# Wider tile slots, product corrections issued before the norm, and head weights applied by TensorE

## The chip, the cores and the metric

One NeuronCore of a Trainium2 chip runs the whole kernel in one launch. The metric is the device time of an execution in microseconds (us). Engines are named as the profile does: PE (TensorE matmuls), PEld (its weight loads), DVE (VectorE), ACT (ScalarE), POOL (GpSimd), SP (the queue that issues most DMAs). L260 is line 260 of the kernel before.

## The reference, cut to what matters

Two blocks of a transformer, then a third with other attention and a mixture of experts; 512 tokens, width 1024, all in float32. What the change touches is the normalisation that opens most stages, and the index scores of the sparse attention (`dsa_mixer`):

```python
def layer_norm(x, g, b):
    mu = jnp.mean(xf, axis=-1, keepdims=True)
    var = jnp.mean(jnp.square(xf - mu), axis=-1, keepdims=True)
    return (xf - mu) * lax.rsqrt(var + LN_EPS) * g + b
...
# sparse attention, block of 128 queries: 8 index heads of width 64
logits = jax.nn.relu(jnp.einsum('bthd,bsd->bths', qib, ki))
score = jnp.einsum('bths,bth->bts', logits, wb)
score = jnp.where(causal[None], score, -jnp.inf)
_, idx = lax.top_k(score, topk)          # topk = 128 of 512 keys
# softmax attention (8 heads of 128, 2 of keys and values) over those keys alone
```

## The kernel before, in words

Activations are kept transposed, eight tiles of 128 channels by 512 tokens. A float32 value is split into two rounded parts, `hi` and `lo`, and a product is made of three matmuls (`mm3`, L260 to L262: hi by hi, hi by lo, lo by hi). Weights come by DMA into `wr`, ACT casts them to `wh` (L237) and DVE, or POOL where the caller says so, subtracts to get `wl` (L238). Both are rings of six tiles. Everything else lies in slots of one pool, `a` (`t()`, 53 slots, 2 x 258 x 4 = 2064 bytes rounded up to a multiple of 32, 2080), small things in `s`, and PSUM has eight banks `p`.

The stages are: feed-forward (`ffn`), mixer, feed-forward, per-layer embedding (`ple`), twice over; then the third block (`nsa` and the experts). The mixers are `ab` (convolution and state space) and `c_mixer` (sparse attention). Six of these stages (ab, ffn, ple, c_mixer, ffn, ple) open with `first_products`: the first four products of the stage are made from values that are multiplied by the gain, but not normalised yet, together with two more columns (hence 258), while DVE works out mean and deviation. `normed` (L402 to L405) then normalises the eight tiles: two DVE operations L402, ACT's L403 and cast L404, DVE's L405 for the low part. Lines L434 (ACT) and L435 to L437 (DVE) correct the four products by the rows of mean and deviation. In the code `normed` is called inside the loop over k, ahead of the corrections. Below, T is the time at which the last matmul of the first products of a site ends.

In `c_mixer` the index queries `qi` (four tiles, two heads in each) and index keys `ki` go through `rope` (a shuffle L959, three elementwise operations L961 to L963, of which POOL makes the first, `engs[0]`). `index()` then makes for j = 3, 2, 1 the scores of 128 queries against 128(j+1) keys: eight matmuls of 64 rows (L1029, even heads on the upper half of the rows, odd heads on the lower), ACT's relu (L1031), and DVE multiplies by the head's weight and adds up (L1033, L1035), and adds the causal mask (L1036). Then 16 rounds of MAX and MATCH_REPLACE (L1042, L1043) over the three score tiles find the top 128, while PE makes the products of ten heads (`product`). `probs` (L1117 to L1134) makes the softmax, and L1557 transposes it. The lows of the last seven head weights and of the first four `cout` weights are made by POOL.

The build's scheduler sets the order of the instructions on each engine; an engine works through its own list in that order, and a waiting instruction holds up all behind it.

Of the kernel before, what the change touches and what calls it, by code (L numbers as in the profile page):

```python
# [18 lines left out]
P = 128  # L19
# [28 lines left out]
V_LNG, V_LNB, V_CONV, V_S5D, V_BGLU, V_NMIX, V_NFFN, NVEC = 0, 48, 96, 108, 112, 116, 124, 132  # L48
C_ID, C_TT, C_TRI, C_CM, C_SGN, C_INVA, C_INVI, C_SINA, C_SINI, C_N = 0, 128, 256, 384, 512, 513, 514, 515, 516, 576
C_I32, C_BASE, C_TOK, C_I128 = 640, 672, 736, 768  # L50
SLOTS, RING, S5_STEP, HALF = 53, 6, 2, 258
CAP, NCOL, NPAIR, NEXT = 64, 32, 16, 16
SLOPES = [float(np.float32(2.0 ** (-8.0 * i / 16))) for i in range(1, 17)]

# [85 lines left out]
class K:  # L140
    def __init__(self, ctx, tc, A, out, stop=None, taps=None):
        self.nc, self.tc, self.A, self.out, self.stop, self.taps = tc.nc, tc, A, out, stop, taps or {}
        nc = tc.nc
        self.n = self.rooms = 0
        self.act = ctx.enter_context(tc.tile_pool(name="act", bufs=1))
        self.ps = ctx.enter_context(tc.tile_pool(name="ps", bufs=1, space=PSUM))
        self.dram = ctx.enter_context(tc.tile_pool(name="dram", bufs=1, space=bass.MemoryType.DRAM))
        self.const = self.act.tile([P, CONST_COLS], F32, name="const", tag="const", bufs=1)
        self.vec = self.act.tile([P, NVEC], F32, name="vec", tag="vec", bufs=1)
        self.ident = self.const[:, C_ID:C_ID + P]  # L150
        self.ones = self.act.tile([P, P], F32, name="ones", tag="ones", bufs=1)
        nc.vector.memset(self.ones, 1.0)
        self.half_pi = self.act.tile([P, 1], F32, name="half_pi", tag="half_pi", bufs=1)
        nc.vector.memset(self.half_pi, math.pi / 2)
        self.vec_hi, self.vec_lo = (self.act.tile([P, V_CONV], F32R, name=n, tag=n, bufs=1) for n in ("vec_hi", "vec_lo"))
        self.background = iter(())

    def begin(self):

        nc, A = self.nc, self.A  # L160
        X, H = [self.t() for _ in range(DT)], self.pairs()
        raw = [self.wide() for _ in range(4)]
        hi, lo = ([self.act.tile([P, 1024], F32R, name=self.nm(t), tag=t, bufs=RING) for _ in range(4)] for t in ("whi", "wlo"))

        def load(t, src):
            with self.after(self.loaded):
                nc.sync.dma_start(t, src)
            self.loaded = self.mark()

        def x(d):  # L170
            load(X[d], A["xT"][d])
            nc.scalar.copy(H[d][0], X[d])
            nc.gpsimd.tensor_tensor(H[d][1], X[d], H[d][0].bitcast(F32), ALU.subtract)

        def w(n, h):
            c = slice(h * S, h * S + S)
            load(raw[n][:, c], A[("w1", "w3")[n % 2]][0, n // 2][:, c])
            nc.scalar.copy(hi[n][:, c], raw[n][:, c])
            nc.vector.tensor_tensor(lo[n][:, c], raw[n][:, c], hi[n][:, c].bitcast(F32), ALU.subtract)

        self.loaded = self.mark()
        x(0)
        w(0, 0)
        w(1, 0)
        x(1)
        w(2, 0)
        w(3, 0)
        x(2)
        x(3)
        x(4)  # L190
        for n in range(4):
            w(n, 1)
            if n < 3:
                x(5 + n)
        with self.after(self.mark()):
            nc.gpsimd.dma_start(self.vec, A["vec"])
            nc.gpsimd.dma_start(self.const, A["const"])
            nc.gpsimd.tensor_copy(self.vec_hi, self.vec[:, :V_CONV])
            nc.gpsimd.tensor_tensor(self.vec_lo, self.vec[:, :V_CONV], self.vec_hi.bitcast(F32), ALU.subtract)
        return X, H, list(zip(hi, lo))  # L200

# [12 lines left out]
        return self.act.tile([P, 1024], F32, name=self.nm("wr"), tag=tag, bufs=2 if tag == "wraw2" else 4)  # L214

    def sm(self, n, dt=F32, p=P):
        t = self.act.tile([P, 64], dt, name=self.nm("s"), tag="s", bufs=34)
        return t[:p, :n]

    def old(self, j):  # L220
# [155 lines left out]

    def halves(self, t):

        return t.rearrange("p (h c) -> p h c", c=HALF)[:, :, :256]

    def gained(self, y, g, b=None):

        nc = self.nc
        if b is None:
            hi, lo = self.t(F32R), self.t(F32R)
            hv, lv, yv = hi, lo, y
        else:
            hi, lo = self.t(F32R, (P, 2 * HALF)), self.t(F32R, (P, 2 * HALF))
            hv, lv, yv = self.halves(hi), self.halves(lo), y.rearrange("p (h c) -> p h c", c=256)
            for t, v in ((hi, self.vec_hi), (lo, self.vec_lo)):  # L390
                nc.gpsimd.tensor_copy(t[:, 256:HALF], v[:, g:b + 1:b - g])  # L391
        gain = self.vec[:, g:g + 1]
        nc.scalar.activation(hv, yv, AF.Copy, scale=gain)  # L393
        nc.vector.scalar_tensor_tensor(lv, yv, gain, hv.bitcast(F32), op0=ALU.mult, op1=ALU.subtract)
        return hi, lo
# [12 lines left out]
    def first_products(self, ws, norm):  # L408

        nc = self.nc
        Y, G, st, g, b = norm
        first, second = [self.bank() for _ in ws], [self.bank() for _ in ws[::2]]
        place = lambda i: second[i // 2][:, i % 2 * 256:i % 2 * 256 + 256]
        for k in range(DT):
            s = slice(k * P, (k + 1) * P)
            hi, lo = G[k]
            for i, w in enumerate(ws):
                l = (w[0][:, s], w[1][:, s])  # L420
                self.mm3(first[i][:, :HALF], l, (hi[:, :HALF], lo[:, :HALF]), k == 0, k == DT - 1)
                self.mm3(place(i), l, (hi[:, HALF:HALF + 256], lo[:, HALF:HALF + 256]), k == 0 and i % 2 == 0, k == DT - 1 and i % 2 == 1)
            self.last_mm = self.mark()
            if k == 0:
                self.loaded = self.mark()
            if k == 1:
                rm = self.result(self.rstd(self.sums(st, range(4), True), 4, 1e-5, True))
            if k == 4:
                rows = [self.spread(c) for c in rm]
                H = self.normed(Y, rows, g, b)  # L430
        res = []
        for i in range(len(ws)):
            c, t = self.sm(2), self.t()
            nc.scalar.copy(c, first[i][:, 256:HALF])  # L434
            nc.vector.tensor_tensor(t[:, :256], first[i][:, :256], rows[0][:, :256], ALU.mult)  # L435
            nc.vector.tensor_tensor(t[:, 256:], place(i), rows[0][:, 256:], ALU.mult)
            nc.vector.scalar_tensor_tensor(t, rows[1], c[:, 0:1], t, op0=ALU.mult, op1=ALU.add)  # L437
            res.append((t, c[:, 1:2]))
        return res, H

    def pairs(self):
        return [(self.t(F32R), self.t(F32R)) for _ in range(DT)]
# [533 lines left out]
    def c_mixer(self, X, H):  # L976
# [9 lines left out]
        def dense(w):  # L986
            o = self.bank()
            self.dense(o, w, H)
            return o

        for _ in self.rounds([self.rope(lambda j=j: first[j] if j < 4 else dense(cw(j)), ri, sh_i, P, (nc.gpsimd, nc.vector), qi, j) for j in range(5)], 1):
            pass
        ki = qi.pop()

# [26 lines left out]
        def index():  # L1021
            for j in (3, 2, 1):
                n = (j + 1) * P
                acc = self.t()[:, :n]
                for h in range(8):
                    o = self.bank()
                    rs = slice(64 * (h % 2), 64 * (h % 2) + 64)
                    q = qi[h // 2]
                    nc.tensor.matmul(o[:, :n], q[rs, j * P:(j + 1) * P], ki[rs, :n], start=True, stop=True)  # L1029
                    r = self.t()  # L1030
                    nc.scalar.activation(r[:, :n], o[:, :n], AF.Relu)  # L1031
                    if h == 0:
                        nc.vector.tensor_scalar(acc, r[:, :n], wi[j][:, h:h + 1], None, op0=ALU.mult)  # L1033
                    else:
                        stt(acc, r[:, :n], wi[j][:, h:h + 1], acc, op0=ALU.mult, op1=ALU.add)  # L1035
                tt(acc[:, n - P:n], acc[:, n - P:n], cm, ALU.add)  # L1036
                bias[j] = acc
                yield
            for i in range(16):
                for acc in bias[:0:-1]:  # L1040
                    m8 = self.sm(8)
                    nc.vector.max(m8, acc)  # L1042
                    nc.vector.match_replace(acc, m8, acc, -3e38)  # L1043
                yield
            for acc in bias[:0:-1]:
                nc.vector.tensor_scalar(acc, acc, -2.9e38, NEG, op0=ALU.is_gt, op1=ALU.mult)
# [5 lines left out]

        def product():
            if lead:
                ws.append(cw(5 + lead.pop(0), nc.gpsimd))
            return dense(ws.pop(0))

        lead = list(heads[3:])
# [30 lines left out]
            self.tap("dsa", [self.merge(x) for x in att])  # L1089
        self.early = self.mark()  # L1090
        X = [self.fetch(("res", d)) for d in range(DT)]
        return self.mix_out(X, "cout", att, 4, nc.gpsimd)

    def merge(self, x):
        t = self.t()
# [911 lines left out]
```

## Time and profile before

| | us |
|---|---|
| median of 3 runs (2834.48 to 2843.33) | 2836.78 |
| profiled execution | 2834.75 |
| its span, first to last instruction | 2833.0 |
| PE busy in it | 2701.3 (95%) |
| DVE, ACT, POOL busy | 1539.5, 997.9, 292.5 |

The span is what the profile covers; the 1.75 us outside it belong to the execution's own time. PE is busy for 95% of the span, so time is to be gained or lost where PE waits, where its clock falls, or in the pace of its matmuls.

### The profile page before, as it was taken

The page shows a single profiled execution, that of the slowest core. Times are in us where ns is not written, and L with a number is a line of the kernel's source. Part 1 is how long each engine was busy: PE and PEld are TensorE (multiplying, and loading weights), DVE is VectorE, ACT ScalarE, POOL GpSimd, SP SyncE. Part 2 cuts the span into 40 slices and gives each one's busy share as a digit, 9 for nine tenths or more (in the row PEclk, how much of TensorE's full clock was granted, in tenths as well). Part 3 has the DMA queues.
Part 4 walks back from the last instruction along what each step waited for, and adds up shares of the span by engine and source line. Part 5 has one row for each costly group of instructions (what it writes and reads, how often), then busy time and mean ns, then how long its engine had stood idle before and what let it go on. Part 6 is the DMA issues. An engine that isn't in the chain of part 4 may idle for free. (4 is left out here: it accounts for less than half of the span.)

```text
span 2833.0 us, 34920 instructions
## 1 busy us (share of the span) xinstructions
PE 2701.3 (95%) x13283; PEld 2100.0 (74%) x13283; DVE 1539.5 (54%) x2880; ACT 997.9 (35%) x1652; POOL 292.5 (10%) x357
## 2 busy tenths in 40 slices
PE   9999989999999999999977999999989999969996
PEld 7877878888888878888866688888877777754443
DVE  6856374574333574333589673333677666543435
ACT  5322243444222363222342552222456544322111
POOL 2101001100000000000028000000014222010000
PEclk9999999999999999999999999999999999989998
DMA  6434225523232223222221123232233222669994
GB/s 217 149 113 143 88 69 167 181 76 113 93 95 89 96 93 97 95 92 91 81 104 60 64 84 98 92 102 83 79 110 117 77 87 72 221 220 361 396 401 159
DMA packets 123817, 370.01 MB, mean 131 GB/s; under 512 B 14592, under 2 KB 14656, under 8 KB 123648
## 3 DMA queue, kind: packets, MB, share of 16 engines
q1 hardware_dynamic: 112688, 333.10, 35.3%
q0 software_dynamic: 10384, 33.61, 3.2%
q8 instruction: 105, 1.72, 0.3%
q10 hardware_dynamic: 576, 1.05, 0.1%
q14 instruction: 64, 0.52, 0.1%
HBM read 343.32 MB, written 24.39 MB: 130 GB/s over the span
## 5 line engine op out<-in xcount | busy, mean ns | idle before, releaser
L260 PE MATMUL p<-a,wh 128*128 128x512 f32 (+2 forms) x3200 | 1229.9, 385 | 13.9 <-DVE a L435 13.7
L262 PE MATMUL p<-a,wl 128*128 128x512 f32 (+2 forms) x3200 | 1222.5, 382 | 0.0
L261 PE MATMUL p<-a,wh 128*128 128x512 f32 (+2 forms) x3200 | 1220.1, 382 | 1.1 <-DVE a L405 1.1
L237 ACT CAST wh<-wr 128x1024 fp32r<-128x1024 f32 (+2 forms) x399 | 408.1, 1029 | 1072.5 <-PE p L261 755.2
L260 PEld LDWEIGHTS p<-a,wh 128*128 128x128 f32 x3200 | 603.1, 189 | 148.7 <-ACT a L540 14.5
L261 PEld LDWEIGHTS p<-a,wh 128*128 128x128 f32 x3200 | 604.0, 189 | 127.2 <-DVE a L405 1.9
L262 PEld LDWEIGHTS p<-a,wl 128*128 128x128 f32 x3200 | 603.2, 188 | 126.5 <-issue 1.7
L238 DVE TENSOR_TENSOR wl<-wr,wh 128x1024 fp32r<-128x1024 f32 (+2 forms) x388 | 468.8, 1212 | 327.8 <-ACT wh L237 319.0
L488 DVE TENSOR_TENSOR a<-a,p 128x512 f32<-128x512 f32 x84 | 57.7, 687 | 270.1 <-PE p L262 251.2
L498 DVE SCALAR_TENSOR_TENSOR a<-p,a 128x512 f32<-128x512 f32 x96 | 66.4, 691 | 203.9 <-PE p L262 203.7
L391 POOL CAST a<-vec_hi 128x2 fp32r<-128x2 f32 x48 | 16.4, 342 | 1142.2 <-PE p L262 576.5
L255 DVE TENSOR_TENSOR a<-a,a 128x512 fp32r<-128x512 f32 x128 | 87.2, 689 | 13.6 <-ACT a L254 13.6
L1124 ACT ACTIVATE a<-a,s 128x256 f32<-128x256 f32 (+3 forms) x128 | 67.2, 526 | 75.0 <-DVE s L1122 74.7
L776 POOL DMA_DIRECT2D spill<-a x76 | 42.7, 563 | 487.5 <-DVE a L552 112.4
L254 ACT CAST a<-a 128x512 fp32r<-128x512 f32 x128 | 78.4, 621 | 21.3 <-DVE a L552 10.5
L402 DVE TENSOR_TENSOR a<-a,a 128x512 f32<-128x512 f32 x96 | 61.2, 686 | 20.0 <-ACT a L374 20.0
L1836 PE MATMUL p<-we,a 128*64 128x512 f32 x288 | 63.7, 592 | 0.0
L1875 PE MATMUL p<-a,sel 128*128 128x512 f32 x256 | 61.9, 397 | 0.1
L393 ACT ACTIVATE a<-a,vec 128x512 fp32r<-128x512 f32 x56 | 40.6, 724 | 60.1 <-DVE a L498 28.9
L1859 ACT ACTIVATE a<-p,wgt 128x512 fp32r<-128x512 f32 x32 | 22.0, 687 | 106.2 <-PE p L1857 102.9
L1117 DVE CUSTOM_DVE_ANT_0 a<-p,a 128x256 f32<-128x256 f32 (+3 forms) x120 | 50.4, 462 | 10.6 <-PE p L1273 10.1
L1875 PEld LDWEIGHTS p<-a,sel 128*128 128x128 f32 x256 | 47.3, 188 | 11.8 <-issue 0.8
(439 smaller groups left out, 2466.2 us busy)
## 6 DMA issues: line engine op xcount, KB each, us to landing
wr<-in_w_dram SPq DMA_DIRECT2D x204, 512.0 KB
we<-in_wgu_dram SPq DMA_DIRECT2D x72, 512.0 KB
wr<-in_w_dram SPq DMA_DIRECT2D x64, 448.0 KB
a<-in_wgu_dram SPq DMA_DIRECT2D x112, 256.0 KB
spill<-a POOLq DMA_DIRECT2D x76, 256.0 KB, 3.4
a<-spill SPq DMA_DIRECT2D x76, 256.0 KB
we<-in_wd_dram SPq DMA_DIRECT2D x36, 512.0 KB
wr<-in_win_dram SPq DMA_DIRECT2D x31, 512.0 KB
```

The source lines that it names most:

```text
L237: nc.scalar.copy(hi[:, :n], raw[:, :n])
L238: (low or nc.vector).tensor_tensor(lo[:, :n], raw[:, :n], hi[:, :n].bitcast(F32), ALU.subtract)
L254: self.nc.scalar.copy(hi[:, :n], x)
L255: (low or self.nc.vector).tensor_tensor(lo[:, :n], x, hi[:, :n].bitcast(F32), ALU.subtract)
L260: mm(o, l[0], r[0], start=start, stop=False)
L261: mm(o, l[0], r[1], start=False, stop=False)
L262: mm(o, l[1], r[0], start=False, stop=stop)
L402: nc.vector.tensor_tensor(y, y, row, op)
L498: nc.vector.scalar_tensor_tensor(Y[d], o, 0.5, Y[d], op0=ALU.mult, op1=ALU.add)
L1124: nc.scalar.activation(s[x], s[x], AF.Exp, bias=nm[:, x:x + 1], accum_out=z[:, x:x + 1])
L1836: nc.tensor.matmul(o[CAP * i:CAP * i + CAP], xT[k // 4][:, a:a + CAP], wg[k], start=k == 0, stop=k == DT - 1)
L1875: nc.tensor.matmul(o, sels[b][:n, j * P:(j + 1) * P], y[h][i][:n], start=b + i == 0, stop=i == 1 and b == len(blocks) - 1)
```

## The change

Three edits in one. First, tiles: the second half of a gained tile moves from column 258 to column 264 (`BEHIND`), so a slot of `a` grows to 2 x 264 x 4 = 2112 bytes (a multiple of 64), `a` loses one slot (52), `s` four buffers (30), and two odd small tiles are padded. Second, `normed` is called at the end of `first_products`, behind the corrections. Third, in `index()` ACT makes diagonal matrices of the head weights (eight scalings of the identity for each j), PE multiplies each relu tile by its diagonal and adds all eight up in one PSUM bank, adds the mask by one more matmul, and ACT copies the sum out. With it, the index ropes run on DVE alone, and DVE makes the lows of two more head weights and of the four `cout` weights that POOL made.

```diff
-SLOTS, RING, S5_STEP, HALF = 53, 6, 2, 258
+SLOTS, RING, S5_STEP, HALF, BEHIND = 52, 6, 2, 258, 264
...
-        t = self.act.tile([P, 64], dt, name=self.nm("s"), tag="s", bufs=34)
+        t = self.act.tile([P, 64], dt, name=self.nm("s"), tag="s", bufs=30)
...
-            hi, lo = self.t(F32R, (P, 2 * HALF)), self.t(F32R, (P, 2 * HALF))
+            hi, lo = (self.t(F32R, (P, 2 * BEHIND)) for _ in range(2))
...
-                self.mm3(place(i), l, (hi[:, HALF:HALF + 256], lo[:, HALF:HALF + 256]), k == 0 and i % 2 == 0, k == DT - 1 and i % 2 == 1)
+                self.mm3(place(i), l, (hi[:, BEHIND:BEHIND + 256], lo[:, BEHIND:BEHIND + 256]), k == 0 and i % 2 == 0, k == DT - 1 and i % 2 == 1)
...
                 rows = [self.spread(c) for c in rm]
-                H = self.normed(Y, rows, g, b)
...
             res.append((t, c[:, 1:2]))
-        return res, H
+        return res, self.normed(Y, rows, g, b)
...
-        for _ in self.rounds([self.rope(lambda j=j: first[j] if j < 4 else dense(cw(j)), ri, sh_i, P, (nc.gpsimd, nc.vector), qi, j) for j in range(5)], 1):
+        for _ in self.rounds([self.rope(lambda j=j: first[j] if j < 4 else dense(cw(j)), ri, sh_i, P, (nc.vector, nc.vector), qi, j) for j in range(5)], 1):
...
-                acc = self.t()[:, :n]
+                acc, total, dgs = self.t()[:, :n], self.bank()[:, :n], []
+                for h in range(8):
+                    if h % 4 == 0:
+                        dgs.append(self.t())
+                    nc.scalar.activation(dgs[-1][:, h % 4 * P:h % 4 * P + P], self.ident, AF.Copy, scale=wi[j][:, h:h + 1])
+
+                def weigh(h, r):
+                    nc.tensor.matmul(total, dgs[h // 4][:, h % 4 * P:h % 4 * P + P], r[:, :n], start=h == 0, stop=False)
+
+                last = None
...
                     nc.scalar.activation(r[:, :n], o[:, :n], AF.Relu)
-                    if h == 0:
-                        nc.vector.tensor_scalar(acc, r[:, :n], wi[j][:, h:h + 1], None, op0=ALU.mult)
-                    else:
-                        stt(acc, r[:, :n], wi[j][:, h:h + 1], acc, op0=ALU.mult, op1=ALU.add)
-                tt(acc[:, n - P:n], acc[:, n - P:n], cm, ALU.add)
+                    if last:
+                        weigh(*last)
+                    last = h, r
+                weigh(*last)
+                nc.tensor.matmul(total[:, n - P:n], self.ident, cm, start=False, stop=True)
+                nc.scalar.copy(acc, total)
...
-                ws.append(cw(5 + lead.pop(0), nc.gpsimd))
+                ws.append(cw(5 + lead.pop(0), nc.gpsimd if len(lead) < 5 else None))
...
-        return self.mix_out(X, "cout", att, 4, nc.gpsimd)
+        return self.mix_out(X, "cout", att, 4)
```

What it does to the order shows on three engines. The first place is DVE at the first `ple`, around the end of its first products. Before, the corrections (L435 to L437, which read the product banks `p`) stand behind the last low parts L405 and three weight lows L238:

```order
L238 TENSOR_TENSOR wl_7968<-wr_7966,wh_7967 128x1024
L238 TENSOR_TENSOR wl_8008<-wr_8006,wh_8007 128x1024
L405 TENSOR_TENSOR a_7704<-a_5262,a_7703 128x512
L238 TENSOR_TENSOR wl_8048<-wr_8046,wh_8047 128x1024
L405 TENSOR_TENSOR a_7706<-a_5264,a_7705 128x512
L435 TENSOR_TENSOR a_7820<-p_7517,a_7675 128x256
L436 TENSOR_TENSOR a_7820<-p_7521,a_7675 128x256
L435 TENSOR_TENSOR a_7826<-p_7518,a_7675 128x256
L437 SCALAR_TENSOR_TENSOR a_7820<-a_7684,s_7819,a_7820 128x512
L436 TENSOR_TENSOR a_7826<-p_7521,a_7675 128x256
```

In the changed kernel (the corrections are now L434 to L436) they stand behind the twelfth L402, and all eight L405 come after the fourth product has been read:

```order
L402 TENSOR_TENSOR a_5256<-a_5256,a_7684 128x512
L402 TENSOR_TENSOR a_5258<-a_5258,a_7684 128x512
L402 TENSOR_TENSOR a_5260<-a_5260,a_7675 128x512
L402 TENSOR_TENSOR a_5262<-a_5262,a_7675 128x512
L434 TENSOR_TENSOR a_7764<-p_7517,a_7675 128x256
L435 TENSOR_TENSOR a_7764<-p_7521,a_7675 128x256
L435 TENSOR_TENSOR a_7770<-p_7521,a_7675 128x256
L436 SCALAR_TENSOR_TENSOR a_7764<-a_7684,s_7763,a_7764 128x512
L434 TENSOR_TENSOR a_7770<-p_7518,a_7675 128x256
L434 TENSOR_TENSOR a_7776<-p_7519,a_7675 128x256
L436 SCALAR_TENSOR_TENSOR a_7770<-a_7684,s_7769,a_7770 128x512
L435 TENSOR_TENSOR a_7776<-p_7522,a_7675 128x256
```

The corrections moved ahead of all L405 and of the remaining L402; the banks are read earlier, the low parts are made later.

The second place is ACT at the first feed-forward stage that opens with `first_products`. Before, the first casts L404 of the normalised tiles stand ahead of L434, which reads the product banks:

```order
L404 CAST a_5098<-a_4558 128x512
L403 ACTIVATE a_4643<-a_4643,vec 128x512
L404 CAST a_5100<-a_4599 128x512
L404 CAST a_5102<-a_4643 128x512
L403 ACTIVATE a_4686<-a_4686,vec 128x512
L434 COPY s_5226<-p_4924 128x2
L434 COPY s_5232<-p_4925 128x2
L404 CAST a_5104<-a_4686 128x512
L403 ACTIVATE a_4729<-a_4729,vec 128x512
L434 COPY s_5238<-p_4926 128x2
L434 COPY s_5244<-p_4927 128x2
```

In the changed kernel the same copies (now L433) come first, with four weight casts L237 among them, and the first L404 follows:

```order
L403 ACTIVATE a_4686<-a_4686,vec 128x512
L403 ACTIVATE a_4729<-a_4729,vec 128x512
L433 COPY s_5170<-p_4924 128x2
L237 CAST wh_5357<-wr_5356 128x1024
L433 COPY s_5176<-p_4925 128x2
L433 COPY s_5182<-p_4926 128x2
L237 CAST wh_5387<-wr_5386 128x1024
L433 COPY s_5188<-p_4927 128x2
L237 CAST wh_5427<-wr_5426 128x1024
L237 CAST wh_5457<-wr_5456 128x1024
L404 CAST a_5194<-a_4558 128x512
L404 CAST a_5196<-a_4599 128x512
```

No cast L404 now stands ahead of the copy that has to wait for the last of the four products; the number of casts and copies is the same.

The third place is PE where the index scores begin, for j = 3 (`a_10923` is `ki`, `p_...` the bank of each head). Before, the eight products of 64 rows follow one another, two heads to each tile of queries:

```order
L1029 MATMUL p_11097<-a_10923,a_10864 128x512
L1029 MATMUL p_11102<-a_10923,a_10864 128x512
L1029 MATMUL p_11107<-a_10923,a_10871 128x512
L1029 MATMUL p_11112<-a_10923,a_10871 128x512
L1029 MATMUL p_11117<-a_10923,a_10878 128x512
L1029 MATMUL p_11122<-a_10923,a_10878 128x512
```

In the changed kernel (they are now L1037) a matmul with a diagonal (L1030, 128 rows, all into the bank `p_11097`) stands behind each from the second on:

```order
L1037 MATMUL p_11108<-a_10923,a_10864 128x512
L1037 MATMUL p_11112<-a_10923,a_10864 128x512
L1030 MATMUL p_11097<-a_11110,a_11098 128x512
L1037 MATMUL p_11117<-a_10923,a_10871 128x512
L1030 MATMUL p_11097<-a_11114,a_11098 128x512
L1037 MATMUL p_11122<-a_10923,a_10871 128x512
L1030 MATMUL p_11097<-a_11119,a_11098 128x512
```

Alternate heads no longer stand next to each other, except the first two; eight L1030 and one mask matmul are new for each j.

## Rows read from the trace of the kernel before

**Rows 1.** The page: span; busy us, share and instructions by engine.
```profile
span 2833.0 us, 34920 instructions
...
PE 2701.3 (95%) x13283; PEld 2100.0 (74%) x13283; DVE 1539.5 (54%) x2880; ACT 997.9 (35%) x1652; POOL 292.5 (10%) x357
```

**Rows 2.** Waits of PE: line, what released it, us in total, times, longest.
```profile
PE p L1557 <- DVE a L1134: 18.8, 2, 18.2
PE p L1029 <- DVE s L1012: 15.7, 1, 15.7
PE p L260 <- DVE a L435: 13.7, 2, 6.9
PE p L794 <- ACT a L868: 9.3, 1, 9.3
...
PE p L1297 <- ACT a L1291: 7.7, 3, 3.6
...
PE p L312 <- DVE a L304: 0.3, 1, 0.3
```

**Rows 3.** Windows: stretch, length, busy us and count by engine, PEclk, DMA share, GB/s.
```profile
424.60:428.00 3.40, 3.35 (x12) 2.75 (x13) 2.98 (x6) 2.14 (x4) 0.00 (x0) 0.51 0.01 2
627.00:638.00 11.00, 11.00 (x52) 8.89 (x51) 11.00 (x18) 9.01 (x15) 0.00 (x0) 1.00 0.31 104
1009.10:1015.00 5.90, 5.84 (x14) 4.63 (x15) 5.90 (x12) 1.35 (x2) 0.00 (x0) 0.50 0.37 133
2162.70:2169.50 6.80, 6.80 (x36) 5.20 (x37) 3.61 (x15) 3.27 (x11) 0.83 (x1) 0.56 0.27 77
```

**Rows 4.** Windows, PE alone, in two long stretches of 128x512 products.
```profile
361.35:384.49 23.14, 23.14 (x102) 1.00 0.21 69
1383.62:1406.97 23.35, 23.35 (x102) 1.00 0.30 92
```

**Rows 5.** Groups by form: count, busy us, mean ns, idle before.
```profile
L260 PE MATMUL p<-a,wh 128*128 128x512 f32 x2816 | 1118.2, 398 | 13.9 <-DVE a L435 13.7
...
L237 ACT CAST wh<-wr 128x1024 fp32r<-128x1024 f32 x328 | 342.0, 1050 | 822.3 <-PE p L261 602.8 <-issue 196.4 <-PE p L262 5.2
...
L404 ACT CAST a<-a 128x512 fp32r<-128x512 f32 x48 | 28.9, 615 | 0.1
```

**Rows 6.** Windows, L1029 alone, its eight 384-column products (j = 2).
```profile
1477.90:1480.50 2.60, 2.55 (x16) 1.24 (x12) 1.00 1.01 410
```

**Rows 7.** Windows, L1074 alone: two heads, 128 rows, 128 to 512 columns.
```profile
1538.50:1542.90 4.40, 4.37 (x16) 2.42 (x15) 1.00 0.38 119
```

**Rows 8.** Timeline of DVE at the first `ple`: start, us, operation, count.
```profile
1009.26 0.42 DVE L435 TENSOR_TENSOR a<-p,a 128x256 f32<-128x256 f32 x1
1009.59 0.75 DVE L437 SCALAR_TENSOR_TENSOR a<-a,s,a 128x512 f32<-128x512 f32 x1
1010.25 0.42 DVE L436 TENSOR_TENSOR a<-p,a 128x256 f32<-128x256 f32 x1
```

**Rows 9.** Timeline of PE at the last first product of `c_mixer`.
```profile
1437.38 0.28 PE L262 MATMUL p<-a,wl 128*128 128x256 f32 x1
1437.50 0.39 PE L260 MATMUL p<-a,wh 128*128 128x512 f32 x1
```

**Rows 10.** Timeline of DVE in `c_mixer`.
```profile
1455.41 0.67 DVE L963 TENSOR_TENSOR a<-a,a 128x512 f32<-128x512 f32 x1
1456.00 1.77 DVE L962 TENSOR_TENSOR a<-a,a 128x512 f32<-128x512 f32 x1
...
1472.37 0.37 DVE L1012 TENSOR_SCALAR s<-p 128x8 f32<-128x8 f32 x4
...
1501.96 1.02 DVE L1042 MAX8 s<-a 128x8 f32<-128x256 f32 x2
```

**Rows 11.** Timeline of DVE at the start of the softmax.
```profile
1555.91 1.21 DVE L238 TENSOR_TENSOR wl<-wr,wh 128x1024 fp32r<-128x1024 f32 x1
1557.05 0.15 DVE L1122 TENSOR_SCALAR s<-s 128x4 f32<-128x4 f32 x1
...
1559.56 0.18 DVE L1130 RECIPROCAL s<-s 128x4 f32<-128x4 f32 x1 [1.23 <-ACT a L1124]
```

More of the change, by code (lines that the diff above doesn't have):

```diff
@@ L148, in __init__ @@
         self.const = self.act.tile([P, CONST_COLS], F32, name="const", tag="const", bufs=1)
-        self.vec = self.act.tile([P, NVEC], F32, name="vec", tag="vec", bufs=1)
+        self.vec = self.act.tile([P, 144], F32, name="vec", tag="vec", bufs=1)
         self.ident = self.const[:, C_ID:C_ID + P]
@@ L152, in __init__ @@
         nc.vector.memset(self.ones, 1.0)
-        self.half_pi = self.act.tile([P, 1], F32, name="half_pi", tag="half_pi", bufs=1)
+        self.half_pi = self.act.tile([P, 16], F32, name="half_pi", tag="half_pi", bufs=1)[:, :1]
         nc.vector.memset(self.half_pi, math.pi / 2)
@@ L195, in begin @@
         with self.after(self.mark()):
-            nc.gpsimd.dma_start(self.vec, A["vec"])
+            nc.gpsimd.dma_start(self.vec[:, :NVEC], A["vec"])
             nc.gpsimd.dma_start(self.const, A["const"])
@@ L377, in halves @@
     def halves(self, t):
-        return t.rearrange("p (h c) -> p h c", c=HALF)[:, :, :256]
+        return t.rearrange("p (h c) -> p h c", c=BEHIND)[:, :, :256]
     def gained(self, y, g, b=None):
```

## Prediction

> **What bounds the kernel now.** I read the page first: PE is busy for 2701.3 of 2833.0 us [rows 1], so the kernel is bound by PE, and time can go or come in three ways only: PE waits, PE's clock falls, or its products change their pace. The waits of PE come next [rows 2]. Four of them lie in stages that the change touches: 18.2 us at L1557 and 15.7 us at L1029, both in `c_mixer` and both ended by DVE; 13.7 us at L260 behind DVE's L435, in two waits of 6.9 (the two `ple`); and 9.3 us at L794 behind ACT's L868 (ab). The feed-forward openings have no row there: between 627 and 638 us PE is busy for all 11.00 us [rows 3]. Last, the windows with the granted clock [rows 3]: after a long wait PE starts at the lower of its two levels, 1.2 GHz (0.50 between 1009.1 and 1015.0, behind the `ple` wait). A wait of 3.6 us at L1297 [rows 2] was enough for that: 6.8 us at 0.56 follow it.
>
> **Tiles.** No instruction is added; at most the pace of the 128x512 products changes, of which there are 3 x 2816 = 8448 [rows 5]. Between two long undisturbed stretches it differs little: 100 starts in 23.14 and in 23.35 us, 231.4 against 233.5 ns [rows 4]. A 2080-byte slot is 32.5 times 64, so of the slots before every second one begins on a multiple of 64 already; if that alone made a product fast, starts would come at two paces within a stretch. If all products came down to the better stretch, from a middle of 232.4, that would be 8448 x 1.0 ns = -8.4 us; if they don't care, 0. I take the middle, -4. A gain beyond any row I leave to a rival. The Trainium skill, SBUF — State Buffer, Operand start alignment, asks of an operand only that it start at a multiple of its element size. By that alone, this term would be 0 and the sum 4 us higher. No row here shows aligned weights, so I keep the -4.
>
> **Corrections ahead of the norm.** The same instructions in another order at six sites. On DVE twelve corrections come first, eight of 0.33 us from start to start and four of 0.66 [rows 8], then the rest of the norm. On ACT the copy L434 of the last product comes before the first cast L404. T is the end of a site's first products.
> *ple, two sites.* PE waits because its next products need banks that L435 and L436 read only behind all low parts. In the changed order they are read from T - 1 to T + 4, while PE has 48 products of the projection (48 x 0.232 = 11.1 us) which don't need the norm. Each site gets back the 6.86 us and half of the 5.9 us at half clock, 2.9. What is late next: the gate's products need the normalised tiles and a bank that ACT's copy L540 empties; that copy now stands behind all eight L404, which end near T + 12, so a wait of some 1 us stays. 2 x (6.86 + 2.9 - 1) = -17.5 us (-14 if the rest is 2.8 us, -19.5 if nothing stays).
> *ffn, two sites.* Here the order costs. PE's first product behind T needs the first L404, which now stands behind the four copies and four weight casts of 1.05 us [rows 5]. The first of the four products is complete at T - 2.2 (three times six matmuls at 0.12 [rows 9] come after it), so: copy and cast to T - 1.0; two copies and a cast to T + 0.4; the last copy to T + 0.6; two casts to T + 2.5; L404 (0.6) [rows 5] to T + 3.1. Before, PE had no wait there; now it has 3.1 us. Whether the clock falls is open: after 3.6 us it did, at a cost of 0.44 x 6.8 = 3.0 us [rows 3]. I take half of that: 2 x (3.1 + 1.6) = +9.4 us (+4 if only half the casts get in the way, +12.4 with the full clock price).
> *ab.* PE waits for L868, and it stays behind all eight L404 on ACT. On DVE the corrections begin at T - 1.6 (twelve L402 stand ahead of them, four follow) and take 5.3 us; five L405 and four L402, 0.6 us each from start to start as L963 [rows 10], put the last L402 at T + 9.1; then L403, L404 and L868 on ACT, 0.6 to 0.8 each [rows 5] by the cast, give T + 11.2, against the 9.3 us of before: +1.9 us (0 to +4). The lower clock behind this wait exists already, 3.4 us at 0.51 [rows 3].
> *c_mixer* has it too, but what PE loses there lies ahead of DVE's rope and is in the next part.
>
> **Index scores.** T is 1437.6 [rows 9]. What ends the stage is DVE's chain: ropes, scores, 16 rounds of MAX, softmax, L1557.
> Ropes: DVE's part of a rope was stretched beside POOL, 1.77 us for L962 against 0.67 for the same work in L963 [rows 10]. Now four operations of 0.6 make one, 2.4 us; five make 12. They begin behind the last low part (T - 1.6 + 5.3 for the corrections + 12 x 0.6 for the rest of the norm + 1.5 for two short weight lows + 0.4 for ACT's share = T + 12.8) and three weight lows of 1.14 [rows 11]: the index queries and keys are ready at T + 28.2 = 1465.8, before at 1472.6: -6.8.
> Scores: for j = 3, 2, 1 PE gets eight L1030 of 512, 384 and 256 columns over 128 rows, and a mask matmul. Two heads of L1074, 2560 columns, took 4.40 us, 1.72 ns a column [rows 7]: 0.88, 0.66, 0.44 us each. L1029 took 2.60 us for 8 x 384 columns, 0.85 ns a column [rows 6], half of that, in pairs of upper and lower rows. In the new order a matmul over all rows stands between the partners, so I price each at the full 1.72; the other bound is 0.85. The Trainium skill, TensorE: Matmul & The Clock Gate, Part 3, has tiles in different row groups run together, while matmuls start and end in program order. By that rule the pairs are gone too; no run here shows a split pair. ACT's eight scalings are priced at 0.3 us (a cast of four times the columns takes 0.6 [rows 5]), 2.4 for each j, and as they stand behind the previous sum's copy PE waits for them. So: j = 3, 1465.8 + 3.3 (DVE's L1012, scalings, first relu) + 14 x 0.88 + 0.2 for the mask + 0.6 for the copy = 1482.2; j = 2, + 2.8 + 14 x 0.66 + 0.2 = 1494.4; the first head's 24 products, + 5.6 = 1500.0; j = 1, + 3.3 + 14 x 0.44 + 0.6 = 1510.1. Before, DVE's steady rounds began at 1501.96 [rows 10], with the first MAX of j = 1; in the new list the same MAX stands there, so +8.1 (not less than -4, if pairs survive and the scalings hide; not more than +11).
> Softmax: DVE makes two weight lows ahead of it that POOL made, 2 x 1.14 = +2.3, and one more between L1122 and the reciprocal, where before 2.5 us pass with two [rows 11]: 3 x 1.14 = 3.4, +1.0. The stage: +11.4 (-1 to +14). PE's 18.2 us shrink, but to nobody's gain, since L1557 waits for DVE.
>
> **Elsewhere** one order differs: L312 behind the second `ple` comes some products later, and its wait of 0.3 [rows 2] could become up to 2; +0.5.
>
> **The sum**, against the profiled execution's 2834.75 (2833.0 span and 1.75 around it): -4 - 17.5 + 9.4 + 1.9 + 11.4 + 0.5 = +1.7, 2836.5 us. The median of the runs shown, 2836.78, is 2.0 us above the profiled one, so this is no change.
>
> **Rivals.**
> *The index costs nothing* (faster). If L1029 keeps its 0.85 ns a column, 8 x (0.44 + 0.33 + 0.22) = 7.9 us go, and if the scalings are done ahead, 5 us more: `c_mixer` ends at -1 instead of +11.4, 2824 us. For it: ACT idles for much of the stage and DVE is rid of 24 multiplications. Against it: the list of ACT has the scalings behind the copy. It decides once the stage costs 1 us or less.
> *The pace falls* (faster). If aligned weights and activations together do what neither shows alone, each ns is worth 8.4 us; 3 ns below the middle give 2814. Against it: only 2 ns lie between the stretches.
> *The feed-forward openings halve the clock* (slower). One mechanism, PE's waits of 3.1 us at the head of ffn and behind each scaling: the clock falls at each for 6.8 us as behind L1297. That is 1.4 x 2 more at ffn, about 3 at each of j = 2 and 1, where PE's waits are 2.8 and 3.4 us, and 2 at ab: +11, 2847. It decides when two thirds of these come, beside a `c_mixer` at its price. The 3.6 us of L1297 speak for it.
> *The change doesn't do what it says*: a `ple` wait that stays, because the gate waits for the last low part (T + 13) instead; +9 at most, on the side of the slower rival and counted there.
>
> **Chances.** Forecast 0.45 (2828 to 2845); index free 0.18; pace 0.12; clock and waits 0.25. About 0.3%, 8.5 us, is what a measurement of this kernel can tell from no change. Faster 0.30, same 0.45, slower 0.25. The range leaves out the far half of the pace rival and the worst of the slower one: 2815 to 2852.
>
> **What would show it.** Right: no L260 behind L435 wait; new PE waits of about 3 us at both ffn openings, released by ACT's L404; L794's wait at 11; the first L1030 some 3 us behind the first L1037; the first MAX of j = 1 near 1506 (1510.1, with +1.9 and +4.7 and -8.8 and half of the -4 ahead of it); L1557's wait around 8. Wrong: L1037 at 0.85 ns a column, products at 230 ns or less in the same two stretches, or a half-clock window behind each ffn opening.

## Result, and the profile after

| | before | after |
|---|---|---|
| median, us | 2839.77 (4 runs, 2834.48 to 2843.33) | 2880.64 (4 runs, 2879.71 to 2884.57) |
| span of the profiled execution | 2833.0 | 2882.6 |
| mean granted clock of PE | 0.979 | 0.970 |

The change makes the kernel slower: ratio 1.0141, 95% interval 1.0122 to 1.0160. The forecast was no change (2836.5, at most 2852). Executions of one kernel differ by some 10 us with the level of PE's clock in a part of ab (last section), so single profiles are compared below stage by stage. The page of the changed kernel, answering to [rows 1]:

```profile
span 2882.6 us, 34964 instructions
...
PE 2759.9 (96%) x13337; PEld 2123.2 (74%) x13337; DVE 1522.4 (53%) x2864; ACT 1007.3 (35%) x1679; POOL 271.5 (9%) x346
```

PE is busy for 58.6 us more and idle for 9 us less. So the time didn't go into waits, and the list of waits shows it (columns as in [rows 2]):

```profile
PE p L793 <- ACT a L867: 11.4, 1, 11.4
PE p L1566 <- DVE a L1143: 10.1, 3, 8.6
PE p L1037 <- DVE s L1011: 9.6, 1, 9.6
...
PE p L260 <- ACT a L404: 8.1, 3, 2.9
...
PE p L1030 <- ACT a L1039: 6.4, 3, 3.4
...
PE p L260 <- ACT a L539: 3.6, 2, 1.9
```

The two waits of 6.9 us behind L435 are gone, those of L1557 (now L1566) and L1029 (now L1037) are shorter; ab's wait grew from 9.3 to 11.4; three waits behind L404, three behind the relu L1039 and two behind L539 are new. Together that is less waiting than before. Yet the same product, found by its place in the program, starts this much later than before (negative: earlier):

| at | us | over the stage |
|---|---|---|
| last product of ab's opening | -0.5 | |
| behind ab's wait | +1.5 | +2.0 |
| first ffn opening: ahead of it, behind it | +3.0, +7.5 | +4.5 |
| first ple: ahead, behind | +6.8, +0.6 | -6.2 |
| `c_mixer`: ahead, behind | -0.1, +54.3 | +54.4 |
| second ffn opening | +54.2, +58.8 | +4.6 |
| second ple: ahead, behind | +58.4, +50.7 | -7.7 |
| opening of the third block | +50.7, +52.8 | +2.1 |
| last product of this kind; end of the span | +52.6, +49.6 | -3.0 |

Nearly all of it is one stage. The windows of PE there, with those behind the ffn and ple waits ahead of them (stretch, length, busy us and count, PEclk, DMA share, GB/s):

```profile
633.60:638.00 4.40, 4.39 (x12) 0.61 0.01 2
1019.30:1025.00 5.70, 5.68 (x18) 0.70 0.81 254
1468.40:1499.80 31.40, 30.23 (x34) 0.50 0.21 67
1499.80:1524.30 24.50, 22.57 (x36) 0.57 0.00 0
1524.30:1530.30 6.00, 6.00 (x25) 0.93 0.01 3
1530.30:1549.80 19.50, 16.14 (x35) 0.63 0.09 27
```

The third to the sixth line are the index scores: j = 3, j = 2, the first head's products, j = 1. In the third PE is busy for 30.23 of 31.40 us, and the clock stands at its lower level, 1.2 GHz, from the first microsecond to the last. Before, the same scores began cold too (L1029 behind its wait), but took 10.1 us for all three j, with the low clock in the first part of j = 3 only (j = 3 and j = 1, columns as in [rows 6], where j = 2 stands):

```profile
1472.55:1477.90 5.35, 5.31 (x18) 2.67 (x20) 0.70 0.74 208
1486.20:1488.35 2.15, 2.10 (x16) 1.56 (x16) 1.00 0.00 0
```

The timeline of PE in the changed kernel shows the price (start, us, operation, count; a float32 matmul leaves two records):

```profile
1468.42 2.08 PE L1037 MATMUL p<-a,a 64*128 64x512 f32 x4 [9.56 <-DVE s L1011]
1471.64 2.07 PE L1030 MATMUL p<-a,a 128*128 128x512 f32 x2 [1.14 <-ACT a L1039]
1473.65 2.07 PE L1037 MATMUL p<-a,a 64*128 64x512 f32 x2
1475.65 2.07 PE L1030 MATMUL p<-a,a 128*128 128x512 f32 x2
```

From 1473.65 on each matmul of 512 columns starts 2.00 us behind the other, 3.9 ns a column; the sum had 1.72. The scores reach DVE when they are copied out (L1045), and DVE's rounds show how late:

```profile
1500.60 0.69 DVE L1051 MAX8 s<-a 128x8 f32<-128x512 f32 x1 [29.76 <-ACT a L1045]
...
1525.02 0.56 DVE L1051 MAX8 s<-a 128x8 f32<-128x384 f32 x1 [22.93 <-ACT a L1045]
...
1550.78 1.02 DVE L1051 MAX8 s<-a 128x8 f32<-128x256 f32 x2 [18.32 <-ACT a L1045]
```

The third row is the first MAX of j = 1, which stood at 1501.96 [rows 10]: 48.8 us later. The softmax adds 4.3 more (two weight lows ahead of it, and three between L1131 and the reciprocal, where in [rows 11] DVE waited for ACT's exponentials):

```profile
1609.22 0.15 DVE L1131 TENSOR_SCALAR s<-s 128x4 f32<-128x4 f32 x1
1609.29 3.48 DVE L238 TENSOR_TENSOR wl<-wr,wh 128x1024 fp32r<-128x1024 f32 x3
1612.69 0.16 DVE L1139 RECIPROCAL s<-s 128x4 f32<-128x4 f32 x1
```

### The profile page after: what moved, and what is told of

Read it like the earlier page. It is cut to its first block, busy times and chain, and to the rows that moved or that the text cites. A ratio compares the mean times of both kernels' runs of the same rounds, so it can differ in the third digit from the quotient of the medians.

```text
span 2882.6 us, 34964 instructions
## 1 busy us (share of the span) xinstructions
PE 2759.9 (96%) x13337; PEld 2123.2 (74%) x13337; DVE 1522.4 (53%) x2864; ACT 1007.3 (35%) x1679; POOL 271.5 (9%) x346
## 3 DMA queue, kind: packets, MB, share of 16 engines
q8 instruction: 105, 1.72, 0.2%
q10 hardware_dynamic: 576, 1.05, 0.1%
## 5 line engine op out<-in xcount | busy, mean ns | idle before, releaser
L237 ACT CAST wh<-wr 128x1024 fp32r<-128x1024 f32 (+2 forms) x399 | 408.0, 1030 | 1079.0 <-PE p L261 775.0
L238 DVE TENSOR_TENSOR wl<-wr,wh 128x1024 fp32r<-128x1024 f32 (+2 forms) x394 | 472.7, 1204 | 327.3 <-ACT wh L237 318.0
L402 DVE TENSOR_TENSOR a<-a,a 128x512 f32<-128x512 f32 x96 | 60.5, 687 | 19.8 <-ACT a L374 19.8
L1051 DVE MAX8 s<-a 128x8 f32<-128x512 f32 (+2 forms) x48 | 24.2, 538 | 71.0 <-ACT a L1045 71.0
L1126 DVE CUSTOM_DVE_ANT_0 a<-p,a 128x256 f32<-128x256 f32 (+3 forms) x120 | 50.5, 461 | 11.0 <-PE p L1282 10.5
```

What stands on the lines that cost most here:

```text
L237: nc.scalar.copy(hi[:, :n], raw[:, :n])
L238: (low or nc.vector).tensor_tensor(lo[:, :n], raw[:, :n], hi[:, :n].bitcast(F32), ALU.subtract)
L402: nc.vector.tensor_tensor(y, y, row, op)
```

## Experiments

Two theories, A and B, were set against each other, and each expectation says what it takes them to be. In `no_index` and `index_only` the question is where the time is lost (A: in the index scores alone), from `pairs` on it is the clock. There, in short, A: the alternation of 64-row and 128-row matmuls itself brings the clock down, or keeps adjacent heads from bringing it up. B: what brings it down is the wait ahead, and these matmuls leave it where they find it.

**One part at a time.** `no_index` is the changed kernel with `index()`, rope engines and weight lows of before; `index_only` the kernel before with those alone; `tiles_only` the kernel before with the wider slots alone.

```diff
# no_index, against the changed kernel
-    nc.scalar.activation(dgs[-1][:, ...], self.ident, AF.Copy, scale=wi[j][:, h:h + 1])
...
+    stt(acc, r[:, :n], wi[j][:, h:h + 1], acc, op0=ALU.mult, op1=ALU.add)
```

> The changed kernel with the whole index part of before (scores added up by DVE, ropes with POOL, lows on POOL): wider tiles and the corrections ahead of the norm alone. Theory A (the 50 us are lost in the index scores alone): the stages ahead of it show +2 at ab, +4.5 at each ffn, -6 at each ple, -2 for the tiles, so -5 us, 2830 to 2838 us, no verdict against before. Theory B (the lost time is also in the new order at c_mixer's opening): 2845 or more. The sum of the prediction without its index term would be 2825.

Measured: 2837.61 us, ratio 0.9996 (0.9984 to 1.0007), as A expected. So are the stages in its profile: ab's wait is 11.4 us, the two ffn openings cost 5.7 and 4.3 us more than before, the two ple 6.1 and 7.7 less, and 2.4 us of that go back at the opening of the third block. The new orders at the six sites nearly cancel out.

> The kernel before with the index part alone. Theory A: +50 to +56 us, 2885 to 2895, with PE at 0.50 through the products of j = 3. Theory B: +20 to +40, since the corrections then stand in their old place. The prediction's term was +11.

Measured: 2890.48 us, 1.0185 (1.0152 to 1.0218), as A expected. The stage alone costs 56.8 us, and its clock is the same (PE alone: stretch, length, busy us and count, PEclk, DMA share, GB/s):

```profile
1473.00:1480.00 7.00, 7.00 (x8) 0.50 0.42 163
1480.00:1500.00 20.00, 20.00 (x23) 0.50 0.00 0
```

So the loss is the index part's, whatever stands ahead of it.

> The kernel before with wider slots and the second half at column 264 alone. The pace of the 128x512 products falls by 0.2 to 0.5 ns, -2 to -4 us; if the tiles do nothing, 0. Products in the two long stretches of before at 230 ns or less would give -15 us or more.

Measured: 2836.23 us, 0.9965 (0.9948 to 0.9982), faster than expected. In its profile the 128x512 products gain 5.4 us against those of before between the first ffn and the last such product, and 3.2 us come behind them, in the experts: 8.6 us. In the first of the two stretches of [rows 4] the same hundred products take as long as before (231.2 ns from start to start), in the second 231.8 ns instead of 233.5. That goes with the slots: in the second stretch every profile with the wider ones has 230.1 to 231.8 ns, `index_only`, with those of before, 233.5. No pace of 230 ns or less is seen in either; which tile it is that pays was not tried.

**Adjacent heads.** `pairs` issues the diagonal matmuls two by two, so that an even and an odd head always follow each other.

```diff
-                    if last:
-                        weigh(*last)
-                    last = h, r
-                weigh(*last)
+                    last.append((h, r))
+                    if h % 2 and h > 1:
+                        weigh(*last.pop(0))
+                        weigh(*last.pop(0))
+                for x in last:
+                    weigh(*x)
```

> The changed kernel, with the diagonal matmuls issued two by two behind the next two index products, so that an even and an odd head always stand next to each other. Theory A (adjacent pairs bring the clock back, as L1029 did within 3.3 us in the kernel before): PE at 1.00 in most of each j, index products at 0.85 ns a column, the three j take some 33 us less, 2845 us. Theory B (the clock stays low whatever the order once PE starts cold, and pairs only halve the index products): PE at 0.50 through j = 3, some 15 us less, 2865 us.

Measured: 2853.34 us, 1.0044 (1.0030 to 1.0059), between the two expected times. The stage costs +13.9 us instead of +54.4. PE alone, in j = 3:

```profile
1477.80:1485.00 7.20, 7.19 (x14) 0.59 0.74 249
1483.00:1484.00 1.00, 1.00 (x2) 0.62 0.73 254
1485.00:1492.00 7.00, 7.00 (x20) 1.00 0.11 43
```

The clock is back some 6 us after a cold start (second line), with the same matmuls in another order. For the clock this is what A expected, of the half of it that says that adjacent heads bring it up. That adjacent heads can do it by themselves, the kernel before shows (0.70 in its j = 3). In `pairs` the diagonal matmuls stand next to each other too, and the clock rose while two of those ran, so what did it there is not shown. Of the 40 us a part is the overlap of the heads, which is back as well (some 15 us by the expectation's own estimate); the run doesn't part it from the clock.

**Scalings ahead.** `early_scalings` has the order of products of the changed kernel, but all 24 scalings ahead of the first.

```diff
-            for j in (3, 2, 1):
+            diag = {}
+            for j in (3, 2, 1):
+                diag[j] = []
+                for h in range(8):
+                    if h % 4 == 0:
+                        diag[j].append(self.t())
+                    nc.scalar.activation(diag[j][-1][:, h % 4 * P:h % 4 * P + P], self.ident, AF.Copy, scale=wi[j][:, h:h + 1])
+            for j in (3, 2, 1):
...
-                acc, total, dgs = self.t()[:, :n], self.bank()[:, :n], []
+                acc, total, dgs = self.t()[:, :n], self.bank()[:, :n], diag[j]
```

> The changed kernel with all 24 scalings issued ahead of the first index product, order of the products as in the changed kernel. So j = 1 starts straight behind the dense products of the first head, at the full clock and without a wait. Theory A (the alternation of 64-row and 128-row float32 matmuls itself lowers the clock): j = 1 falls to 0.50 again though nothing makes PE wait, it takes 14 to 16 us as in the changed kernel, and the time is 2870 to 2880. Theory B (only the wait ahead lowers the clock, and these matmuls merely don't raise it): j = 1 runs at 1.00 and takes about 8 us, 2862 to 2868.

Measured: 2871.96 us, 1.0123 (1.0100 to 1.0145). The clock follows B; the time, of two runs 8 us apart, lies in A's range. The windows of PE in j = 3, 2 and 1, and three starts:

```profile
1484.00:1512.40 28.40, 28.09 (x30) 0.50 0.02 7
1514.30:1526.00 11.70, 11.70 (x31) 1.00 0.00 0
1533.40:1543.00 9.60, 9.57 (x34) 1.00 0.20 55
```

```profile
1484.31 2.08 PE L1033 MATMUL p<-a,a 128*128 128x512 f32 x2 [5.81 <-ACT a L1042]
...
1514.31 0.91 PE L1033 MATMUL p<-a,a 128*128 128x384 f32 x2 [0.58 <-ACT a L1042]
1515.15 0.91 PE L1040 MATMUL p<-a,a 64*128 64x384 f32 x2
```

j = 3 is at the low clock throughout, as in the changed kernel. j = 2 and j = 1 run at the full clock to their end, in the very order that A held for the cause, with waits of 0.6 and 1.0 us near their start. So that order alone doesn't lower the clock, as B has it. In the changed kernel the same j = 2, behind a wait of 1.93 us, fell to the low clock and stayed there:

```profile
1505.30:1523.80 18.50, 18.50 (x25) 0.50 0.00 0
```

In `early_scalings` the clock rose at the turn from j = 3 to j = 2, where the last two diagonal matmuls, the mask and the first two heads follow one another without alternation. What follows a wait counts as well, though. In `pairs` j = 2 stands behind a wait of 1.95 us, in the paired order, and keeps the full clock (behind 2.93 us, in its j = 1, the clock fell):

```profile
1495.93:1503.30 7.37, 7.37 (x25) 1.00 0.00 0
```

These are single executions, so no rule for waits of this length follows. The starts in `early_scalings` also give the full-clock price of a split head: 0.84 us for 384 columns, where 0.66 was in the sum.

**Warm start.** `warm` puts the products of two heads ahead of the index products, where PE waited.

```diff
-        idx = index()
-        for _ in range(2):
-            next(idx)
...
+        idx = index()
...
-            for _ in range(2):
+            for _ in range(0 if n == 0 else 4 if n == 1 else 2):
                 next(idx, None)
```

> The changed kernel with the products of the first two heads issued ahead of the index products, where PE waited 9.6 us; nothing else. Theory B (these matmuls hold the clock where they find it, and it is the wait ahead that decides): j = 3 runs at 1.00, about 17 us instead of 31.4; j = 2 and 1 keep their waits behind the scalings and may fall again; 2852 to 2868. Theory A (the alternation lowers the clock): j = 3 at 0.50 from some microseconds after its start, 2878 to 2886.

Measured: 2881.42 us, 1.0143 (1.0107 to 1.0179), no gain: A's number came, and B's was wrong. Its windows say why:

```profile
1470.00:1477.00 7.00, 7.00 (x31) 1.00 0.42 121
1478.10:1481.30 3.20, 0.05 (x3) 0.98 0.42 149
1481.30:1505.30 24.00, 24.00 (x24) 0.50 0.20 66
```

PE comes in at 1.00, makes the first two heads, waits 3.15 us for the relu behind eight scalings, and comes out at 0.50 for the rest of j = 3. So the wait of 9.6 us need not be there: one of 3 us is as good, and this is what B's number overlooked. The eight scalings take what the sum had for them, 2.4 us (ACT in the changed kernel, j = 3):

```profile
1468.66 2.45 ACT L1027 ACTIVATE a<-const,s 128x128 f32<-128x128 f32 x8 [7.14 <-DVE s L1011]
```

**Both.** `pairs_early` has the order of `pairs` and the scalings of `early_scalings`.

> The kernel pairs with all 24 scalings ahead of the first index product. The waits of PE behind the scalings of j = 2 and 1 (1.95 and 2.93 us) go, and so does the fall of the clock behind the second: 7 to 10 us less than pairs, 2844 to 2847. If ACT's scalings only move their wait to j = 3, 3 us less.

Measured: 2852.22 us, 1.0047 (1.0031 to 1.0062). A miss: the waits of j = 2 and j = 1 fell to 0 and 0.6 us, but the scalings now stand ahead of j = 3, where PE waits 4.1 us for its first relu, and the stage costs +14.7 us, 0.8 more than in `pairs`. The wait only moved.

**Corrections first at the ple alone, and ropes on DVE.**

```diff
# ple_only, against no_index
-    def first_products(self, ws, norm):
+    def first_products(self, ws, norm, late=False):
...
+                H = None if late else self.normed(Y, rows, g, b)
...
-        return res, self.normed(Y, rows, g, b)
+        return res, H or self.normed(Y, rows, g, b)
# ple_rope, against ple_only
-..., ri, sh_i, P, (nc.gpsimd, nc.vector), qi, j)
+..., ri, sh_i, P, (nc.vector, nc.vector), qi, j)
```

> Wider tiles, index as before, corrections ahead of the norm at the two ple alone, norm first at the other four sites. The two ple keep what they won in no_index (some 6 us each), the +2 at ab and the +4.5 at each ffn go: 10 to 13 us less than before, 2827 to 2832 beside 2843. If the ple gain hangs on the other sites' order, as no_index.

> ple_only with the index ropes on DVE alone. By the prediction's rope term the index starts 5 to 7 us earlier, and since DVE's chain sets the end of the stage, the time falls by as much against ple_only: 2821 to 2826. Rival: DVE's scores stay held up by POOL's weight lows, and the whole gain is lost by the first MAX of j = 1.

Measured: 2826.64 us, 0.9958 (0.9941 to 0.9976), and 2818.28 us, 0.9941 (0.9918 to 0.9964). In `ple_only` the ffn openings are back at 0, ab's wait at 9.4, the two ple give 6.1 and 7.7 us, of which 2.2 go back at the opening of the third block. The 8 us between the two are not the rope's: the stage around the index costs -1.9 us against before in `ple_only` and -0.9 in `ple_rope`, and the difference stands already in the state-space part of ab. L1029's wait shrinks by 0.8 us only (15.8 to 15.0). DVE saves the 5.4 us by which POOL's part of the ropes stretched its L962, and makes the five L961 itself, 3.0 us. But POOL, free of the ropes, now makes its weight lows beside them. They stretch three of DVE's operations, which take some 0.7 us elsewhere, by 5.9 us together (DVE, then POOL, in `ple_rope`), where they had cost two operations behind the ropes 4.3:

```profile
1446.07 2.97 DVE L437 SCALAR_TENSOR_TENSOR a<-a,s,a 128x512 f32<-128x512 f32 x1
1449.56 2.86 DVE L962 TENSOR_TENSOR a<-a,a 128x512 f32<-128x512 f32 x1
1452.98 2.20 DVE L963 TENSOR_TENSOR a<-a,a 128x512 f32<-128x512 f32 x1
```

```profile
1446.09 2.40 POOL L238 TENSOR_TENSOR wl<-wr,wh 128x1024 fp32r<-128x1024 f32 x1 [79.65 <-ACT wh L237]
1449.34 5.29 POOL L238 TENSOR_TENSOR wl<-wr,wh 128x1024 fp32r<-128x1024 f32 x2 [0.86 <-ACT wh L237]
```

The rope expectation was a miss. Its rival had named POOL's weight lows, but at the scores: they met the ropes.

**The rest of the ple stall.** `ple_copy` issues three of ACT's copies of the ple projection ahead of the casts of the normalised tiles.

```diff
             nc.scalar.copy(t, a)
             pj.append(t)
+            if d == 2:
+                H = later()
```

> ple_rope with ACT's first three copies of the ple projection issued ahead of the normalised tiles' casts, so that PE finds a free bank for the gate's fifth product. By the reading of the changed kernel the rest of each ple stall is a wait of 1.9 us for that copy and 1.7 us at the low clock behind it: both go at both sites, 7 us less than ple_rope, some 2811 us in a like execution. If the gate then waits for the last low part instead, 0 to 3 us less.

Measured: 2826.00 us, 0.9934 (0.9916 to 0.9952), a miss. At the first ple the wait and the low clock go (first line), which is worth 3.9 us more than in `ple_only`; behind the second, PE now waits for the first tiles of the third block (second line), and all of that is given back:

```profile
1018.00:1028.00 10.00, 10.00 (x45) 1.00 0.58 174
2097.00:2108.00 11.00, 5.56 (x23) 0.78 0.08 24
```

**Sums on PE without the waits.** `tuned_cold` is `ple_rope` with the sums on PE in pairs, the head weights by ACT from the bank, the scalings of j = 3 early and those of the next j between the relus; `tuned` has the two heads ahead as well.

```diff
+            for h in range(8):
+                scaled(3, h)
...
+                    if j > 1:
+                        scaled(j - 1, h)
```

> ple_rope with the index scores on PE, in pairs, head weights by ACT straight from the bank, the scalings of j = 3 ahead and those of the next j between the relus; PE still waits ahead of j = 3. If the clock is what costs, j = 3 starts at 0.50, pairs bring it back within 8 us and no wait takes it away again: the first MAX of j = 1 comes 3 to 8 us later than in ple_rope, 2820 to 2828.

> tuned_cold with the products of two heads ahead of the index products. Theory B: full clock in all three j, 10.5 + 7.9 + 5.3 us of PE, the first MAX of j = 1 earlier than in ple_rope, 2808 to 2816 beside 2818; the sums on PE then cost nothing, as the prediction's rival had it. If it is 2820 or more, the additions on PE are not worth their matmuls even at the full clock.

Measured: 2836.65 us, 0.9973 (0.9955 to 0.9990), and 2823.98 us, 0.9925 (0.9900 to 0.9951). The stage costs +9.6 us against before in `tuned_cold`, -1.3 in `tuned`. In `tuned_cold` the first MAX of j = 1 comes 6.3 us later than in `ple_rope`, as expected, though the median lies above the range. `tuned` doesn't have the full clock throughout, which B expected: PE waits 2.15 us in j = 3, and a part at the low clock follows before it comes back:

```profile
1473.80:1480.00 6.20, 6.20 (x12) 0.72 0.28 85
```

Its time is over B's range, and over the 2820 at which the additions were to be called not worth their matmuls. So the sums on PE cost nothing once PE comes in warm and the heads are paired, and also bring nothing: DVE's rounds begin 1.6 us earlier than in `ple_rope`, counted from the start of the stage. `tuned`, `ple_copy` and `ple_rope` all beat both kernels; their intervals overlap, and no run tells them apart.

## Why the prediction was wrong, step by step

- **Index scores, the step that failed.** "Two heads of L1074, 2560 columns, took 4.40 us, 1.72 ns a column [rows 7]", and "I price each at the full 1.72". Each row of that price was taken at the full clock, and the stage starts behind a wait. The sum had +11.4, measured +54.4. At 1.2 GHz a split head costs 3.9 ns a column; at 2.4 GHz, in `early_scalings`, 2.2. In the sum of this stage the low clock had no term at all, and in the slower rival it was a passing cost of at most 6.8 us at a wait, because behind the three waits that I read PE came back by itself within 3.4 to 6.8 us [rows 3]. In the new order it stays low for 31.4 us; `pairs` shows that the order does it, by giving 40 us back, clock and overlap together, with the same matmuls. With the clock up, the stage would still have been about 23 us worse, not 11. This is an estimate: to the 11.4 come 7.6 us for fourteen matmuls each of 1.05, 0.84 and 0.63 us in place of 0.88, 0.66 and 0.44 (0.84 and 0.63 are steps of `early_scalings`, 1.05 goes on from them), 2.6 us for the later start of the index products, and 1.0 for the softmax. That the partners don't overlap was right: the Trainium skill, TensorE: Matmul & The Clock Gate, Part 3, has matmuls start and end in program order, and the trace agrees, 0.84 us for a split index product of 384 columns and 0.39 us in `pairs` (four in 1.56 us).
- **The place of the ropes** was near: the index products start 4.2 us earlier than before, the sum had 6.8.
- **Softmax**: +4.3, the sum had +3.3.
- **ple**: the mechanism was right, the size not. 6.2 and 7.7 us instead of 2 x 8.8: the rest is a wait for the copy L539, as named, of 1.9 and 1.7 us, not 1, and at the first site behind it the low clock (0.70 between 1019.3 and 1025.0), which I had not put there. At the second site the clock stays up. `ple_copy` shows wait and low clock going together at the first site.
- **ffn**: +4.5 and +4.6, the sum had 4.7 each. The wait is 2.9 us, behind L404, and the clock does fall (0.61). That the size fits is in part luck: the 1.6 us for the clock were the middle between a fall of 3 us and none, and it fell for a shorter time (0.61 over 4.4 us, 1.7 us lost).
- **ab**: +2.0, the sum had 1.9.
- **Elsewhere**: +2.1 at the opening of the third block, the sum had 0.5. It is a wait of 2.1 us behind ACT's L1222, which the kernel before doesn't have, and not a longer one at L312.
- **Tiles**: `tiles_only` has 8.6 us in its profile and 0.9965 in its runs; the sum had 4 and the bound 8.4. In the changed kernel some 5 us are gained between the stages of the table, 3.0 of them behind the last such product. The Trainium skill, SBUF — State Buffer, Operand start alignment, asks for no more than the element size. The Trainium skill says there that this is about legality and not about speed, so the 0 that the prediction took from it did not follow; the measurement decides against 0.
- **Rivals.** That PE's waits behind the scalings halve the clock was the slower rival, and its mechanism was the right one; its price of about 3 us for each fall was not, since it ended each fall after 6.8 us, and it had none at j = 3, behind the longest wait. The rival that the index costs nothing is what `tuned` does, but only in another order.

## What to carry to other kernels

A price per column read at the full clock holds only where the clock is full: before work is moved to PE, look at what stands ahead of it (a wait of 1.9 to 3 us was enough at most places here, though not at every one) and whether the new sequence brings the clock back. A busy PE can stay at half clock for as long as a stage lasts (31.4 us here); the page's share doesn't show it, the windows with the granted clock do. Matmuls over half of the rows belong next to their partner: one over all rows between them cost the overlap here (0.84 us instead of 0.39) and, after a cold start, the clock.

A new order at a shared opening has to be looked at where each stage uses it: the same move won 6 to 8 us where PE waited for banks and cost 4.5 where it waited for nothing.

## What the runs showed of the hardware that was not expected

PE at 1.2 GHz while busy for 28.09 of 28.40 us (`early_scalings`, j = 3), and the same sequence, with 384 columns for 512, at 2.4 GHz for 11.70 us when it was entered at that level: this order holds either level. The 384 columns alone show both too, 18.50 us at 1.2 GHz in the changed kernel. The clock also fell behind waits as short as 1.92 us (first ple) and 2.9 us (ffn). It didn't behind 1.73 us at the second ple, in the same kernel:

```profile
2122.30:2130.00 7.70, 7.65 (x33) 1.00 0.80 265
```

The state-space part of ab runs at either level too, from execution to execution, with PE busy all through. The kernel before, in its profiled execution, and below it `tiles_only`, which changes nothing there but the slots:

```profile
440.00:450.00 10.00, 10.00 (x71) 1.00 0.98 310
470.00:480.00 10.00, 10.00 (x69) 1.00 0.18 54
```

```profile
440.00:450.00 10.00, 10.00 (x64) 0.69 0.97 287
470.00:480.00 10.00, 10.00 (x48) 0.66 0.17 52
```

Over that part `tiles_only` loses 10.7 us to the profile of before, `ple_only` 10.5, and `ple_rope`, with the same slots, 1.5. What decides in an execution which level it is was not found.
